# A two-layer decoder trunk on one core: in the second attention, exponentials issued ahead of copies and maxima in a row, with the groups placed anew

## The chip, the core and the metric

The kernel runs on one core of one Trainium2 chip. A core has a tensor engine (PE, with its weight loads PEld beside it), a vector engine (DVE), a scalar engine (ACT), GpSimd (POOL) and a queue engine (SP) that here issues most of the DMAs. The metric is the device time of one execution in microseconds (us). Three runs of the kernel before took 973.27, 973.38 and 973.73 us; their median, 973.38 us, is the time before.

## What is computed

The program takes 256 tokens of width 1024 through two layers. Each layer has a half-step SwiGLU feed-forward block, a token mixer, and a second half-step block; a vector `c` gives every sub-layer a shift, a scale and a gate. The mixer of layer 0 is a differential attention of 8 heads, that of layer 1 a forgetting attention of 16 heads over keys and values that were computed once before it:

```python
def block(args):                       # layer 0: two score maps per head
    logits = einsum('bqhmd,bkhmd->bhmqk', qb, k) * scale + bias
    p = softmax(where(rel >= 0, logits, -inf))
    w = p[:, :, 0] - lam * p[:, :, 1]
    return einsum('bhqk,bkhe->bqhe', w, v)
...
def block(args):                       # layer 1: one score map per head, and a decay
    logits = einsum('bqhd,bkhd->bhqk', qb, k) * scale + (F_q - F_k)
    p = softmax(where(causal, logits, -inf))
    return einsum('bhqk,bkhd->bqhd', p, v)
...
x = x + 0.5 * g1 * swiglu(h, w_in0, w_out0)
x = x + g2 * mix(h)
x = x + 0.5 * g3 * swiglu(h, w_in1, w_out1)
```

## The kernel before

**Products in three parts.** The stream `x`, the hidden rows and the weights are each kept as a rounded high part and a low part that holds the rest. A product is three matmuls into one bank (`mm3`): high by high, low weight by high, high weight by low. So each 128x1024 piece of weights (`raw`, 512 KB, loaded by SP) passes twice through the vector engines: ACT casts it (`wh<-raw`), and DVE subtracts the high part (`wl<-raw,wh`). There are 360 such pieces. `raw` has 6 buffers, `wh` 6, `wl` 5; a load into a `raw` buffer waits until both have read it, and a new `wh` or `wl` waits until PE has used the piece 6 or 5 places earlier. A second stream, `ada`, gives the shifts, scales and gates: one DVE pass over 128x1024 each.

**What sets the order.** The class `InOrder` (line 54) records what is called on PE, ACT, DVE and SP and keeps each engine's instructions in that order on the chip. It also keeps a rough clock for each engine. When an ACT or DVE call would wait by that clock, it calls a filler first: `fill_act` puts casts there, `fill_dve` subtractions or `ada` blocks. `plainly` (line 69) runs a function with the filler off. `bg`, called after matmuls by `work`, adds casts and subtractions too.

**First attention** (`attention_a`, line 975). Heads go through `group(t)` (line 1086): scores of head t, transposes of the weights of head t-1, values of t-2, and transposes of the output of t-3 on PE, then on ACT and DVE the copies, `exps` (four row maxima on DVE, each with its exponential on ACT), `squares` and `out_split`. `combine(t)` scales and subtracts the two maps (`nl`) before `group(t+1)` transposes them. Between the groups PE gets steps of projections: of the queries and keys, and, for the last three groups, of the output (`OutProj.steps`, three matmuls a step, banks `pw`). `OutProj.finish` (line 828) then does the last two heads and updates `x`.

**Second attention** (`attention_b`, line 1222). Two heads make a pair c; eight pairs go through `group(t)` (line 1320), t from 0 to 9:

- PE: `scores(t)` into two banks `sb`, `values(t-2)` into the second half of `wb`, then `weights_t(t-1)`, six transposes into `wa` and `wb`.
- ACT before the change: the high part of the output of pair t-2 (`obh<-wb`), then the four exponentials of pair t (`d<-d,nmb`), then the copy `wta<-wa` of pair t-1.
- DVE: the four maxima of pair t (`d<-sb,d` with `nmb`), the copy `wtb<-wb`, the low part `obl` of the output.
- `scale(t)` (a reciprocal `rsb` and four multiplications of `d`) is called before the last two steps ahead of `group(t+1)`.

The tiles `d` start as decays: POOL loads each of the 16 from DRAM (`d<-fdram`, line 1240) and adds a causal mask by a second DMA (`d<-tri`, line 1248), which waits for the first. Decays and masks of pairs 0 to 4 are issued ahead, those of pairs 5, 6 and 7 in groups 1, 2 and 3, one behind the other on POOL's queue.

Between the groups PE takes steps from `fills()` (line 1343): first the projections of the last two query tiles (`lq`, banks of the pool `mm`; six matmuls for every two steps, 32 steps), then six rounds of `OutProj.steps` (`pw`, three matmuls a step, 48 steps). `pw` has four banks in the same pool of four: the first two were those of the second-last projection, `pw2` and `pw3` are those of the last one, and so wait until `late_out` has drained it (ACT `lcol<-lq`, DVE `lt<-lq`, ACT `q<-lt`). The tuple of line 1353 says how many steps stand ahead of each group; four more follow the last, and eight are left to `finish`.

Of the kernel before, what the change touches and what calls it, by code (L numbers as in the profile page):

```python
# [10 lines left out]
F32 = mybir.dt.float32  # L11
# [3 lines left out]
ALU = mybir.AluOpType  # L15
# [7 lines left out]
AH = 8  # L23
# [80 lines left out]
def trunk(ctx, tc, a, out):  # L104
# [3 lines left out]
    act = InOrder(tc, nc.scalar, 0.13, 1 / 1200)  # L108
    dve = InOrder(tc, nc.vector, 0.08, 1 / 960)
# [19 lines left out]

    mm = pe.matmul  # L130


    crow = ap_.tile([P, 2, D], F32, tag="ada", name="crow").rearrange("p a b -> p (a b)")
    act.dma_start(crow[:1, :D], a["c"])
# [840 lines left out]
    def attention_a():  # L975
# [21 lines left out]
        op = OutProj(o)  # L997
# [11 lines left out]
        def exps(hd, sb):  # L1009
            g = gs[hd]  # L1010
            nl = []
            nm = kp.tile([P, 4], F32, tag="nm", name=f"nm{hd}")
            sm = kp.tile([P, 4], F32, tag="sm", name=f"sm{hd}")
            for m in range(2):
                s = sb[m]
                n_ = cp_.tile([P, 384], F32, tag=f"hidh{4 + 2 * (hd % 2) + m}", name=f"nl{hd}_{m}")
                nl.append(n_)
                for qt, (c0, w) in enumerate(QT):
                    cc = 2 * m + qt
                    dve.tensor_tensor_reduce(  # L1020
                        n_[:, c0:c0 + w], s[:, c0:c0 + w], g[:, S - w:], -0.125, BIG,
                        ALU.add, ALU.min, accum_out=nm[:, cc:cc + 1])
                    act.activation(n_[:, c0:c0 + w], n_[:, c0:c0 + w], AF.Exp,
                                   bias=nm[:, cc:cc + 1], scale=-1.0,
                                   accum_out=sm[:, cc:cc + 1])
            st[hd], sms[hd] = nl, sm
# [54 lines left out]
        def out_split(hd, pz):  # L1081
            oh, ol = o[hd]
            act.activation(oh, pz, AF.Identity, scale=subg)
            dve.scalar_tensor_tensor(ol, pz, subg, oh.bitcast(F32), op0=ALU.mult, op1=ALU.subtract)

        def group(t):

            hs, hw, hv, ho = (h if 0 <= h < AH else None for h in (t, t - 1, t - 2, t - 3))
            bank = bbank(f"po{t}") if hv is not None or ho is not None else None
            sb = scores(hs) if hs is not None else None  # L1090
            pw = weights_t(hw) if hw is not None else None
            if hv is not None:
                values(hv, bank[:, :256])
            if ho is not None:
                out_t(ho, bank[:, 256:])
            if hw is not None:
                wt = cp_.tile([P, 384], F32, tag=f"hidh{8 + hw % 2}", name=f"wt{hw}")
                act.copy(wt, pw[:, :384])
                st[hw] = wt
            if hs is not None:  # L1100
                exps(hs, sb)
            if hv is not None:
                squares(hv, bank[:, :256])
                inv_rms(hv)
            if ho is not None:
                out_split(ho, bank[:, 256:])

        def after(t):
            if t < AH:
                combine(t)  # L1110
            if 0 <= t - 2 < AH:
                scale_o(t - 2)

# [36 lines left out]
    op, rest = attention_a()  # L1150
# [71 lines left out]
    def attention_b():  # L1222
# [27 lines left out]
        r = late_pairs("wq", q[:2], None, AF.Exp)  # L1250
# [5 lines left out]
        op = OutProj(o)  # L1256
# [56 lines left out]
        def out_split(c, po):  # L1313
            if c % 2 == 0:
                o_tiles(c // 2)
            oh, ol = o[c]
            act.copy(oh, po)
            return lambda: dve.tensor_tensor(ol, po, oh.bitcast(F32), op=ALU.subtract)

        def group(t):  # L1320

            cs, cw, cv = (c if 0 <= c < NP else None for c in (t, t - 1, t - 2))
            sb = [sbank(f"sb{t}_{m}") for m in range(2)] if cs is not None else None
            ta = abank(f"wa{t}") if cw is not None else None
            tb = bbank(f"wb{t}") if cw is not None or cv is not None else None
            if cs is not None:
                scores(cs, sb)
            if cv is not None:
                values(cv, tb[:, 256:])
            if cw is not None:  # L1330
                weights_t(cw, ta, tb)
            low = out_split(cv, tb[:, 256:]) if cv is not None else None
            if cs is not None:
                exps(cs, sb)
            if cw is not None:
                weights_out(cw, ta, tb)
            if low:
                low()
            if cw is not None and t + 4 < NP:
                decay(t + 4)  # L1340
                masked(t + 4)
# [8 lines left out]
                    yield  # L1350

        fill = fills()
        for t, n in enumerate((3, 9, 8, 8, 8, 8, 7, 7, 6, 4)):
            for i in range(n):
                if 1 <= t <= NP and i == n - 2:
                    scale(t - 1)
                next(fill)
            group(t)
# [5 lines left out]
    op, rest = attention_b()  # L1364
# [132 lines left out]
```

## Time and profile before

| what | value |
|---|---|
| time, median of 3 runs | 973.38 us (973.27 to 973.73) |
| the profiled execution's own time | 973.79 us |
| its span, first to last instruction | 972.0 us |
| instructions | 20418 |
| granted PE clock | 0.997 of full speed |
| read from HBM | 264.75 MB |
| first attention's last groups and steps | about 280 to 300 us |
| second attention's groups | about 730 to 775 us |

The span lies within the profiled execution's time; 1.8 us of that time are outside it, and that execution was 0.4 us longer than the median run. A row of the timeline gives the start, the duration, the engine, the line (99 for all that `InOrder` records), the operation, the tiles out<-in, the shape, how many, and in brackets the idle time just before it with what ended it. Matmuls overlap, so the distance of two starts says more than a duration. SP, ACT or POOL followed by q is an engine's queue.

### The profile page before, as it was taken

The page shows a single profiled execution, that of the slowest core. Times are in us where ns is not written, and L with a number is a line of the kernel's source. Part 1 is how long each engine was busy: PE and PEld are TensorE (multiplying, and loading weights), DVE is VectorE, ACT ScalarE, POOL GpSimd, SP SyncE. Part 2 cuts the span into 40 slices and gives each one's busy share as a digit, 9 for nine tenths or more (in the row PEclk, how much of TensorE's full clock was granted, in tenths as well). Part 3 has the DMA queues.
Part 4 walks back from the last instruction along what each step waited for, and adds up shares of the span by engine and source line. Part 5 has one row for each costly group of instructions (what it writes and reads, how often), then busy time and mean ns, then how long its engine had stood idle before and what let it go on. Part 6 is the DMA issues. An engine that isn't in the chain of part 4 may idle for free.

```text
span 972.0 us, 20418 instructions
## 1 busy us (share of the span) xinstructions
PE 959.7 (99%) x8076; PEld 933.5 (96%) x8076; DVE 819.8 (84%) x1372; ACT 551.8 (57%) x894; POOL 74.6 (8%) x110
## 2 busy tenths in 40 slices
PE   8999999999999999999999999999999999999997
PEld 7999999998999999999998999999998899999997
DVE  6989979889999999888889988988977799555575
ACT  4466635566777654545576545445567776455432
POOL 0000200000112000000000000000044214300000
PEclk9999999999999999999999999999999999999999
DMA  9998899967866699888959799988899537977651
GB/s 360 415 356 267 326 369 344 344 228 265 314 226 229 204 376 381 306 271 311 326 197 370 289 340 338 361 295 317 315 301 224 146 111 233 262 157 267 187 153 44
DMA packets 73825, 270.32 MB, mean 278 GB/s; under 512 B 9673, under 2 KB 14577, under 8 KB 63618
## 3 DMA queue, kind: packets, MB, share of 16 engines
q1 hardware_dynamic: 66016, 259.69, 76.0%
q0 software_dynamic: 7424, 9.02, 4.3%
q8 instruction: 63, 1.03, 0.4%
q10 hardware_dynamic: 290, 0.32, 0.1%
q14 instruction: 32, 0.26, 0.1%
HBM read 264.75 MB, written 2.66 MB: 275 GB/s over the span
## 4 chain that ended last, share of the span: by engine, by line
PE 94%; DVE 3%; issue 1%; ACT 1%; POOL 0%; ACTq 0%; DVEq 0%; POOLq 0%
PE po L99 25%; PE pg L99 21%; PE pu L99 21%; PE pf L99 5%; PE pv L99 5%; PE lp L99 4%; PE pqk L99 3%; PE pw L99 3%; PE pk L99 1%; PE lq L99 1%; DVE wl L99 1%; PE wb L99 1%; DVE HL L99 1%; PE s L99 1%; PE sb L99 1%
## 5 line engine op out<-in xcount | busy, mean ns | idle before, releaser
L99 ACT CAST wh<-raw 128x1024 fp32r<-128x1024 f32 (+1 forms) x360 | 347.5, 975 | 208.4 <-PE pu L99 83.6
L99 DVE TENSOR_TENSOR wl<-raw,wh 128x1024 fp32r<-128x1024 f32 (+1 forms) x360 | 398.7, 1126 | 70.7 <-ACT sg L99 19.2
L99 DVE CUSTOM_DVE_ANT_0 ada<-ada,cact,vecs 128x1024 f32<-128x1024 f32 x160 | 203.6, 1279 | 0.4 <-DMA ada<-in_ada 0.4
L99 PE MATMUL pg<-HH,wl 128*128 128x256 f32 x608 | 168.0, 276 | 0.2 <-DVE wl L99 0.2
L99 PE MATMUL pg<-HH,wh 128*128 128x256 f32 x608 | 168.0, 276 | 0.0
L99 PE MATMUL pu<-HH,wh 128*128 128x256 f32 x608 | 167.9, 276 | 0.0
L99 PE MATMUL pg<-HL,wh 128*128 128x256 f32 x608 | 167.9, 276 | 0.0
L99 PE MATMUL pu<-HL,wh 128*128 128x256 f32 x608 | 167.9, 276 | 0.0
L99 PE MATMUL pu<-HH,wl 128*128 128x256 f32 x608 | 167.9, 276 | 0.0
L99 PE MATMUL po<-hidh,wh 128*128 128x256 f32 x528 | 145.7, 276 | 0.0
L99 PE MATMUL po<-hidh,wl 128*128 128x256 f32 x528 | 145.7, 276 | 0.0
L99 PE MATMUL po<-hidl,wh 128*128 128x256 f32 x528 | 145.7, 276 | 0.0
L99 PEld LDWEIGHTS pg<-HH,wh 128*128 128x128 f32 x608 | 114.1, 188 | 0.7 <-issue 0.6
L99 PEld LDWEIGHTS pg<-HH,wl 128*128 128x128 f32 x608 | 114.1, 188 | 0.5 <-DVE wl L99 0.4
L99 PEld LDWEIGHTS pu<-HH,wl 128*128 128x128 f32 x608 | 114.1, 188 | 0.0
L99 PEld LDWEIGHTS pu<-HL,wh 128*128 128x128 f32 x608 | 114.1, 188 | 0.0
L99 PEld LDWEIGHTS pu<-HH,wh 128*128 128x128 f32 x608 | 114.1, 188 | 0.0
L99 PEld LDWEIGHTS pg<-HL,wh 128*128 128x128 f32 x608 | 114.1, 188 | 0.0
L99 PEld LDWEIGHTS po<-hidh,wh 128*128 128x128 f32 x528 | 99.1, 188 | 0.0
L99 PEld LDWEIGHTS po<-hidh,wl 128*128 128x128 f32 x528 | 99.1, 188 | 0.0
L99 PEld LDWEIGHTS po<-hidl,wh 128*128 128x128 f32 x528 | 99.1, 188 | 0.0
L99 ACT CAST hidh<-hf 128x512 fp32r<-128x512 f32 x44 | 27.3, 621 | 41.8 <-DVE hf L99 41.6
(224 smaller groups left out, 1866.2 us busy)
## 6 DMA issues: line engine op xcount, KB each, us to landing
raw<-in_win SPq DMA_DIRECT2D x176, 512.0 KB, 6.6
ada<-in_ada SPq DMA_DIRECT2D x79, 1024.0 KB, 7.1
raw<-in_wout SPq DMA_DIRECT2D x48, 384.0 KB, 5.4
raw<-in_wout SPq DMA_DIRECT2D x48, 320.0 KB, 5.6
raw<-in_wqk SPq DMA_DIRECT2D x16, 512.0 KB, 5.5
raw<-in_wo SPq DMA_DIRECT2D x16, 512.0 KB, 6.0
raw<-in_wlast SPq DMA_DIRECT2D x16, 512.0 KB, 4.3
raw<-in_wv SPq DMA_DIRECT2D x8, 512.0 KB, 6.9
```

Source lines behind the costliest of these rows:

```text
L99: return self.tc.keep_in_program_order(f(*args, **kw))
```

## The change

Three things change, all in what is called when; no operation is added or taken away.

- **Second attention, order within a group.** The exponentials and maxima of pair t are called first and with both fillers off, then the copies `wta` and `wtb`, then the output's high and low part. So ACT has the exponentials ahead of `wta` and `obh`, and no subtraction stands between the four maxima.
- **Second attention, places.** The steps ahead of groups 0 to 9 go from (3, 9, 8, 8, 8, 8, 7, 7, 6, 4) to (3, 9, 7, 7, 8, 8, 7, 7, 7, 5). Both make 68.
- **First attention, last head.** `exps`, `combine` and `out_split` of head 7 are called with the fillers off.

```diff
+    def plain(f, *args):
+
+        r = []
+        act.plainly(lambda: dve.plainly(lambda: r.append(f(*args))))
+        return r[0]
...
             if hs is not None:
-                exps(hs, sb)
+                plain(exps, hs, sb) if hs == AH - 1 else exps(hs, sb)
...
             if ho is not None:
-                out_split(ho, bank[:, 256:])
+                plain(out_split, ho, bank[:, 256:]) if ho == AH - 1 else out_split(ho, bank[:, 256:])
 
         def after(t):
             if t < AH:
-                combine(t)
+                plain(combine, t) if t == AH - 1 else combine(t)
...
             oh, ol = o[c]
             act.copy(oh, po)
-            return lambda: dve.tensor_tensor(ol, po, oh.bitcast(F32), op=ALU.subtract)
+            dve.tensor_tensor(ol, po, oh.bitcast(F32), op=ALU.subtract)
...
-            low = out_split(cv, tb[:, 256:]) if cv is not None else None
             if cs is not None:
-                exps(cs, sb)
+                plain(exps, cs, sb)
             if cw is not None:
                 weights_out(cw, ta, tb)
-            if low:
-                low()
+            if cv is not None:
+                out_split(cv, tb[:, 256:])
...
-        for t, n in enumerate((3, 9, 8, 8, 8, 8, 7, 7, 6, 4)):
+        for t, n in enumerate((3, 9, 7, 7, 8, 8, 7, 7, 7, 5)):
```

Three places show what this does to the instructions.

**Around group 4 of the second attention, PE.** `pw0` to `pw2` are banks of the output projection, `sb4` the scores of pair 4, `wb4` and `wa4` its group's other banks. Before:

```order
L99 MATMUL pw1_9706<-obl0_9579,wh_9347 128x256
L99 MATMUL pw2_9707<-obh0_9578,wh_9347 128x256
L99 MATMUL pw2_9707<-obh0_9578,wl_9418 128x256
L99 MATMUL pw2_9707<-obl0_9579,wh_9347 128x256
L99 MATMUL pw0_9705<-obh0_9578,wh_9347 128x256
L99 MATMUL pw0_9705<-obh0_9578,wl_9418 128x256
L99 MATMUL pw0_9705<-obl0_9579,wh_9347 128x256
L99 MATMUL sb4_0_9733<-kT_6358,q2_9230 128x128
L99 MATMUL sb4_1_9734<-kT_6358,q2_9230 128x128
```

And PE there in the changed kernel:

```order
L99 MATMUL pw1_9712<-obl0_9593,wh_9347 128x256
L99 MATMUL sb4_0_9721<-kT_6358,q2_9230 128x128
L99 MATMUL sb4_1_9722<-kT_6358,q2_9230 128x128
L99 MATMUL sb4_0_9721<-kT_6358,q2_9230 128x256
L99 MATMUL sb4_1_9722<-kT_6358,q2_9230 128x256
L99 MATMUL wb4_9724<-wta2_9662,vb_6359 64x256
L99 MATMUL wb4_9724<-wtb2_9663,vb_6359 64x256
L99 MATMUL wb4_9724<-wta2_9662,vb_6359 64x128 x2
L99 MATMUL wa4_9723<-tri_1167,d6_9399 128x128 x3
L99 MATMUL wa4_9723<-tri_1167,d7_9401 128x128
L99 MATMUL wb4_9724<-tri_1167,d7_9401 128x128 x2
L99 MATMUL pw2_9713<-obh0_9592,wh_9347 128x256
```

The whole of group 4 now stands ahead of the first use of `pw2`. Group 3 moved too: six matmuls of the last `lq` projection that stood ahead of it follow it now.

**Pair 7 of the second attention, DVE.** `d14` and `d15` are the two heads' tiles, `nmb7` their maxima (a read of the accumulator follows each), `rsb7` the reciprocal that opens `scale(7)`. Before, from the first maximum on:

```order
L99 ISA d_9678,nmb_9956<-sb_0_9935,d_9678 128x128
L99 ISA nmb_9956 128x1
L99 TENSOR_TENSOR wl<-raw,wh 128x1024
L99 ISA d_9678,nmb_9956<-sb_0_9935,d_9678 128x256
L99 ISA nmb_9956 128x1
L99 ISA d_9680,nmb_9956<-sb_1_9936,d_9680 128x128
L99 ISA nmb_9956 128x1
L99 ISA d_9680,nmb_9956<-sb_1_9936,d_9680 128x256
L99 ISA nmb_9956 128x1
L99 COPY wtb_9971<-wb_9938 128x256
L99 TENSOR_TENSOR obl_9891<-wb_9938,obh_9890 128x256
L99 RECIPROCAL rsb_9987<-smb_9957 128x4
```

DVE of the changed kernel, from the second maximum on:

```order
L99 ISA d_9672,nmb_9947<-sb_0_9929,d_9672 128x256
L99 ISA nmb_9947 128x1
L99 ISA d_9674,nmb_9947<-sb_1_9930,d_9674 128x128
L99 ISA nmb_9947 128x1
L99 ISA d_9674,nmb_9947<-sb_1_9930,d_9674 128x256
L99 ISA nmb_9947 128x1
L99 COPY wtb_9958<-wb_9932 128x256
L99 TENSOR_TENSOR obl_9899<-wb_9932,obh_9898 128x256
L99 TENSOR_TENSOR wl<-raw,wh 128x1024
L99 RECIPROCAL rsb_9984<-smb_9948 128x4
```

The subtraction that stood between the maxima stands between `obl` and the reciprocal. (In pairs 5 and 6 it stands behind the maxima and ahead of `wtb`, in pairs 2 to 4 between `wtb` and `obl`.)

**Head 7 of the first attention, DVE.** `nl_0` and `nl_1` are the two maps, `nm` their maxima, `ss` the sums of squares of an earlier head. Before:

```order
L99 ISA nl_0_3649,nm_3647<-s_0_3630,g_3477 128x128
L99 ISA nm_3647 128x1
L99 TENSOR_TENSOR wl<-raw,wh 128x1024
L99 ISA nl_0_3649,nm_3647<-s_0_3630,g_3477 128x256
L99 ISA nm_3647 128x1
L99 ISA nl_1_3658,nm_3647<-s_1_3631,g_3477 128x128
L99 ISA nm_3647 128x1
L99 ISA nl_1_3658,nm_3647<-s_1_3631,g_3477 128x256
L99 ISA nm_3647 128x1
L99 ISA ada,modall<-ada,cact,vecs 128x1024
L99 ISA modall 128x1
L99 TENSOR_SCALAR ss_3664<-ss_3664 128x2
```

And in the changed kernel:

```order
L99 ISA nl_0_3649,nm_3647<-s_0_3630,g_3477 128x256
L99 ISA nm_3647 128x1
L99 ISA nl_1_3654,nm_3647<-s_1_3631,g_3477 128x128
L99 ISA nm_3647 128x1
L99 ISA nl_1_3654,nm_3647<-s_1_3631,g_3477 128x256
L99 ISA nm_3647 128x1
L99 TENSOR_TENSOR wl<-raw,wh 128x1024
L99 TENSOR_SCALAR ss_3660<-ss_3660 128x2
L99 SCALAR_TENSOR_TENSOR ol_2565<-po_3629,small,oh_2561 128x256
L99 RECIPROCAL rs_3689<-sm_3648 128x4
```

The four maxima are together, the subtraction follows them, and the `ada` block is gone from here: it now stands some 15 us later, behind the last low part `ol` and ahead of the first update of `x`; the subtraction that was ahead of that update follows it.

## The prediction

> **What bounds the kernel now.** I read the busy times first, then PE's list of waits.
>
> ```profile
> PE 959.7 (99%) x8076; PEld 933.5 (96%) x8076; DVE 819.8 (84%) x1372; ACT 551.8 (57%) x894; POOL 74.6 (8%) x110
> ```
>
> PE is busy for 959.7 of the 972.0 us and loses no matmul by the change. Only time in which PE stands can be won, and the change reaches three of the waits in PE's list (us, times, longest):
>
> ```profile
> PE pw L99 <- DVE lt L99: 1.1, 1, 1.1
> PE pw L99 <- DVE nl L99: 0.8, 2, 0.4
> PE wb L99 <- ACT wta L99: 0.6, 1, 0.6
> ```
>
> Together that is 2.5 us, 0.26% of the time. So the question is whether each goes, and what is late next. For scale: about 0.2% (1.95 us) is what a measurement of this kernel can tell from no change.
>
> **Second attention, the wait for `lt`.** PE's timeline, then ACT's and DVE's, around group 3:
>
> ```profile
> 747.44 0.28 PE L99 MATMUL lq<-HL,wh 128*128 128x258 f32 x1
> 748.14 0.28 PE L99 MATMUL pw<-obl,wh 128*128 128x256 f32 x1
> 749.48 0.38 PE L99 MATMUL pw<-obh,wh 128*128 128x256 f32 x1 [1.06 <-DVE lt L99]
> 749.70 0.28 PE L99 MATMUL pw<-obh,wl 128*128 128x256 f32 x1
> ...
> 746.31 0.37 ACT L99 CAST obh<-wb 128x256 fp32r<-128x256 f32 x1 [1.81 <-PE wb L99]
> 746.58 0.41 ACT L99 ACTIVATE d<-d,nmb 128x128 f32<-128x128 f32 x1
> 748.35 0.56 ACT L99 COPY wta<-wa 128x512 f32<-128x512 f32 x1
> 748.81 0.22 ACT L99 COPY lcol<-lq 128x1 f32<-128x1 f32 x2
> ...
> 749.00 0.76 DVE L99 TENSOR_TENSOR lt<-lq,r 128x256 f32<-128x256 f32 x2 [1.30 <-ACT lcol L99]
> 751.01 1.01 DVE L99 TENSOR_SCALAR d<-d,rsb 128x128 f32<-128x128 f32 x4
> ```
>
> The last `lq` matmul ends at 747.72, but ACT reaches `lcol` only at 748.81: `obh` had waited 1.81 us for PE's values, with the exponentials and `wta` queued behind it. `lt` follows, then `pw2`. PE's starts are 1.34 us apart where two of a run are 0.12 apart, and the next distance is 0.22: the wait costs 1.22 + 0.10 = 1.3 us.
>
> Two things remove it. The exponentials no longer queue behind `obh`, and group 3 comes six matmuls (0.7 us) earlier against the same end of `lq`. Its scores start at 743.0, the first exponential runs at 744.3, `wta` 1.77 later (748.35 - 746.58) at 746.1 and `obh` at 746.6. So ACT is idle when `lq` ends; `lcol` runs at about 747.8, `lt` at 748.0. And PE has group 4 to do ahead of `pw2`, over 2 us. Late instead could be the transposes of pair 3 in group 4: their scaling is queued on DVE behind the two `lt`, starts at about 748.8 and ends 1.01 later, at 749.85; PE comes to the second head's transposes at about 750.4. So 0.5 us is spare. Bounds 0 and -1.3; I take **-1.3**.
>
> At nothing I cost the casts. Behind `obh` of groups 2 and 4 two now stand in a row, two times 0.95 us from about 742.2 and 752.6, done 0.2 to 0.4 us ahead of the next exponentials. If that cover goes, the idle second of ACT ahead of `lcol` takes up the first pair, and 1 us of spare in the scaling of pair 5 the other.
>
> **Second attention, the wait for `wta`.** PE stood ahead of group 8:
>
> ```profile
> 762.71 0.37 PE L99 MATMUL pw<-obh,wh 128*128 128x256 f32 x1
> 765.28 0.93 PE L99 MATMUL sb<-kT,q 64*128 64x128 f32 x8
> 766.14 0.43 PE L99 MATMUL wb<-wta,vb 128*64 128x256 f32 x1
> 766.94 0.66 PE L99 MATMUL wa<-tri,d 128*128 128x128 f32 x4
> 767.57 0.37 PE L99 MATMUL pw<-obh,wh 128*128 128x256 f32 x1
> 769.60 0.28 PE L99 MATMUL pw<-obl,wh 128*128 128x256 f32 x1
> 770.51 0.43 PE L99 MATMUL wb<-wta,vb 128*64 128x256 f32 x1 [0.64 <-ACT wta L99]
> ```
>
> The distance 769.60 to 770.51 is 0.91, where a change of kind takes about 0.2: 0.7 us lost. Let T be the start of pair 7's scores. The group takes 767.57 - 765.28 = 2.29, and the seven steps that now follow it 765.28 - 762.71 = 2.57. So group 8 begins at T + 4.86 and its transposes, behind the values (766.94 - 766.14 = 0.80), at T + 5.66. `wta` is ready by T + 3.6, so this wait goes. But DVE is late now:
>
> ```profile
> 759.11 0.41 DVE L99 TENSOR_TENSOR obl<-wb,obh 128x256 fp32r<-128x256 f32 x1
> 759.44 1.21 DVE L99 TENSOR_TENSOR wl<-raw,wh 128x1024 fp32r<-128x1024 f32 x1
> 760.57 0.17 DVE L99 RECIPROCAL rsb<-smb 128x4 f32<-128x4 f32 x1
> 766.29 0.29 DVE L99 CUSTOM_DVE_ANT_0 d<-sb,d 128x128 f32<-128x128 f32 x1
> ```
>
> Maxima start at T + 1.0 (766.29 against 765.28), exponentials at T + 1.35 for 1.77, then `wta` (0.46), `obh` (0.37) and `obl`, at T + 4.0. Ahead of the scaling stand `obl` (0.33 to the next start) and the moved `wl` (1.13): the reciprocal comes at T + 5.45, the scaling 0.2 later; its first head is done at T + 6.15, its second at T + 6.65. PE waits from T + 5.66 about 0.5 for the first, 0.1 for the second, and loses 0.1 on the restart. 0.7 goes and 0.7 comes: **0**, with bounds -0.7 (the wait gone) and +0.5 (half a `wl` later). In groups 2 to 6 the `wl` stands ahead of `obl`, where DVE waits for `obh` anyway, and PE comes 1 us or more after the scaling.
>
> **The masks.** Group 7 begins about 2.0 us earlier (1.3, and two steps of 0.34 less ahead of it), T = 763.3, and its first maximum wants `d14`, mask and all, at 764.3. The mask's issue on POOL and its landing (last figure, us), then the landing of pair 6's masks, and two subtractions:
>
> ```profile
> 760.32 2.47 POOL L1248 DMA_DIRECT2D d<-tri  x2 [2.97 <-DMA d<-fdram]
> d<-tri POOLq DMA_DIRECT2D x2, 128.0 KB, 5.4
> ...
> d<-tri POOLq DMA_DIRECT2D x2, 128.0 KB, 3.6
> ...
> 739.55 1.22 DVE L99 TENSOR_TENSOR wl<-raw,wh 128x1024 fp32r<-128x1024 f32 x1
> ```
>
> Before, it landed at 760.32 + 5.4 = 765.7, 0.6 ahead of its maximum. It waits only for the DMAs ahead of it on POOL's queue, so an earlier PE doesn't bring it. At 765.7 it would be 1.4 us late, and all of that late for PE in group 8. What changes is the weight loads beside these DMAs, since a load is issued when a `wl` ends. The slow mask had one issued 0.3 us behind it (the `wl` of 759.44 ends at 760.65); that `wl` now comes at about 760.5. The `wl` of 739.55 moves to 741.3, so that its load meets less of pair 5's decay, first of the chain. I expect the chain 1 to 2 us earlier and the last mask in 3.6 to 4.5 us, landed between 763 and 764.5: **0**. Bounds 0 and +1.4.
>
> The Trainium skill's page "DMA: Bandwidth & Descriptors", section "Queues, rings and completion order", says that each DMA engine takes turns between its queues a packet at a time; 5.4 against 3.6 us agrees. Its section "Anatomy of one DMA — SWDGE (gpsimd) path" gives 2.0 us and the bytes at 436 GB/s, an estimate of 2.3 us for 128 KB; by that price no mask is late and the sum is the same, but both rows are longer.
>
> **First attention, the wait for `nl`.**
>
> ```profile
> 287.64 0.28 PE L99 MATMUL pw<-ol,wh 128*128 128x256 f32 x1
> 288.33 0.30 PE L99 MATMUL pw<-tri,nl 128*128 128x128 f32 x1 [0.42 <-DVE nl L99]
> 289.02 0.44 PE L99 MATMUL pw<-tri,nl 128*128 128x128 f32 x2 [0.39 <-DVE nl L99]
> ```
>
> Two distances of 0.69, less 0.2 and 0.12 for a change and a run, with a restart inside: 0.95 us lost by the starts, 0.81 by the idle times; I take the starts, on which PE's pace rests. The `wl` between the maxima held ACT's second exponential by its 1.13 us; without it `nl` is 1.1 earlier and both waits go: -0.95. But the `ada` block comes back ahead of the updates of `x`, and their sums run one behind the other on POOL:
>
> ```profile
> 301.18 0.87 DVE L99 SCALAR_TENSOR_TENSOR x<-pw,modall,x 128x256 f32<-128x256 f32 x2
> 302.50 0.49 ACT L99 ACTIVATE HH<-x,modall 128x256 fp32r<-128x256 f32 x1
> 304.72 4.42 POOL L443 TENSOR_TENSOR acc<-acc,sq 128x256 f32<-128x256 f32 x5 [0.53 <-ACT sq L99]
> ...
> 323.26 1.22 DVE L99 TENSOR_TENSOR wl<-raw,wh 128x1024 fp32r<-128x1024 f32 x1
> 325.18 0.28 PE L99 MATMUL pg<-HH,wl 128*128 128x256 f32 x1
> ```
>
> DVE has no gap from the last `ol` to the second update, now with about 1.2 us more in it: that update starts at 301.8 (0.2 later), and ACT's `HH` from it at 302.3 instead of 302.50. The sums, then three `wl`, the rescaling and the rows of `h` follow from there, so this chain gains 0.2 where PE gains 0.95. The `wl` of 323.26 ended at 324.48, 0.7 ahead of its first use; now 324.3 against 324.2. PE waits 0.1 and restarts for 0.1: **-0.75**, with bounds -0.95 and -0.5 (the chain no earlier at all).
>
> **The sum.** -1.3 + 0 + 0 - 0.75 = -2.05. The profiled execution took 973.79 (span 972.0, 1.8 around it) and would take 971.74; it was 0.41 above the median run, so the median goes from 973.38 to **971.3**. Behind both places PE, DVE and ACT have their old order, and buffers that PE frees set their pace, so the gain lasts to the end.
>
> **The rivals.**
>
> - *The mask is late.* The chain of decays and masks keeps its old times, and 1.4 of the gain becomes a wait of DVE's maxima, then of PE's transposes in group 8: 972.7, or between 971.6 and 972.7 in part. For it: a chain on one queue that no engine feeds. Against it: the loads that move. Chance 0.27.
> - *The first attention gives back more*, or group 4 waits for its scaling: half a us to one, 971.9 to 972.3 (I take 971.9, the nearer end). Margins of 0.1 and 0.5 us speak for it. Chance 0.1.
> - *Better:* the group 8 wait goes too, as DVE finds time for the `wl` early; 971.3 - 0.7 = 970.6. Against it: the new order puts it behind `obl`. Chance 0.1.
> - *Slower:* moved weight loads meet two more transfers of the chain, each 1.8 us longer (5.4 - 3.6): landing at 765.7 + 3.6 = 769.3, 5.0 late, 976.3. It decides from a landing of 766.35 on, where the gain of 2.05 is used up, and shows as slower from 768.3. Against it: as many loads as before. Chance 0.04.
> - That the change doesn't do what it says is excluded by the order of the rows.
>
> **How the numbers follow.** The forecast has 0.49, with 0.4 us to either side. Some six in ten of it lie below 971.43, with all of the better case: faster 0.4, slower 0.04, same 0.56. The range goes from the better case to a mask a little later than before: 970.4 to 973.2.
>
> **What would show it.** PE's list without `lt` and `nl`, and `wa` waiting for DVE's `d` instead of `wb` for `wta`, 0.5 to 0.7 us: right. A wait of DVE's `d` for a DMA at group 7, with a mask that lands after 764.5: the first rival. A wait of `pg` for `wl` near 324 above 0.3 us: the second. Wrong in any case: PE still waiting near 748, or new idle time of PE in the last feed-forward.

## The result, and the profile after

| | median | lowest to highest | runs |
|---|---|---|---|
| before, beside the change | 973.82 us | 973.04 to 977.45, and one run of 1369 | 22 |
| changed kernel | 978.87 us | 972.11 to 989.17 | 22 |

The ratio is 1.005 [1.0031, 1.0068]: the change makes the kernel 0.5% slower, where 0.2% faster was forecast, and the time lies outside the range. The runs of 1369 and 989.17 us count as slow and are left out of the ratio. The wide spread of the others belongs to the result: four of them lie below 975.3, 972.11 the lowest, and seven between 981.5 and 985. The profiled execution took 978.58 us, 4.8 more than that of before.

PE's list of waits in the changed kernel (us, times, longest), the lines that the rest goes by:

```profile
PE wb L99 <- DVE obl L99: 2.9, 1, 2.9
...
PE pg L99 <- DVE wl L99: 0.6, 2, 0.4
PE wb L99 <- DVE rsb L99: 0.6, 1, 0.6
PE wa L99 <- DVE d L99: 0.4, 1, 0.4
```

The three waits that the change was to remove are gone. In their place stands one of 2.9 us at group 8 of the second attention and some small ones. The place is best seen as a table by stage, around groups 7 to 9. The columns are the stretch, its length, the busy time of PE, PEld, DVE, ACT and POOL, the granted clock, the DMA share and GB/s. First before, then after:

```profile
764.00:769.00 5.00, 5.00 (x46) 4.23 (x46) 3.96 (x17) 3.69 (x13) 0.00 (x0) 1.00 0.47 71
769.00:772.00 3.00, 2.36 (x23) 1.85 (x21) 1.48 (x6) 1.45 (x7) 0.00 (x0) 1.00 0.48 164
772.00:778.00 6.00, 6.00 (x54) 5.55 (x53) 4.02 (x7) 5.08 (x9) 0.00 (x0) 1.00 0.27 87
```

```profile
764.00:769.00 5.00, 4.38 (x39) 3.72 (x35) 1.99 (x9) 0.51 (x2) 1.11 (x1) 1.00 0.81 161
769.00:772.00 3.00, 0.12 (x2) 0.00 (x0) 1.66 (x9) 3.00 (x11) 0.00 (x0) 0.89 0.01 3
772.00:778.00 6.00, 5.94 (x29) 5.11 (x29) 4.12 (x9) 2.31 (x4) 0.00 (x0) 0.50 0.27 87
778.00:785.00 7.00, 7.00 (x62) 6.48 (x62) 4.23 (x8) 5.02 (x10) 0.73 (x1) 0.99 0.45 144
```

PE stands almost the whole of 769 to 772. Then, although it is busy for 5.94 of 6.00 us, it does 29 matmuls where it did 54: the granted clock is 0.50. What it had stood for is told by DVE's timeline (first a maximum of pair 6, then the first one of pair 7) and by POOL's:

```profile
761.85 0.29 DVE L99 CUSTOM_DVE_ANT_0 d<-sb,d 128x128 f32<-128x128 f32 x1 [1.68 <-DMA d<-tri]
...
768.52 0.29 DVE L99 CUSTOM_DVE_ANT_0 d<-sb,d 128x128 f32<-128x128 f32 x1 [2.57 <-DMA d<-tri]
771.49 0.42 DVE L99 TENSOR_TENSOR obl<-wb,obh 128x256 fp32r<-128x256 f32 x1 [1.33 <-ACT obh L99]
```

```profile
756.43 2.15 POOL L1245 DMA_DIRECT2D d<-fdram  x2
762.64 2.47 POOL L1253 DMA_DIRECT2D d<-tri  x2 [4.05 <-DMA d<-fdram]
```

The first maximum of pair 7 is computed when its mask has landed; behind it come the other maxima, ACT's exponentials, `wta` and `obh`, and the `obl` for which PE waits. The mask was issued at 762.64, when the decays of 756.43 had landed, and needed 5.7 us (the list of transfers gives it as the last figure):

```profile
d<-tri POOLq DMA_DIRECT2D x2, 128.0 KB, 5.7
```

It landed at 768.36. Pair 7's scores began at 763.42, so by PE the maximum was ready to run at 764.42: 3.9 us late. (DVE itself, which pair 6's late mask had held up, was free from 765.95 on.)

To see where the time went I set the start of each matmul of the changed kernel against the matmul of the same number before:

```
at      after - before   what lies between
 277 us   -0.99          start-up, code that the change leaves alone
 290      -2.06          the two waits for nl gone: -1.07
 308      -1.58          PE held up by x at 305:    about +0.5
 326      -0.75          a new wait for wl at 324:  about +0.8
 734      -0.75
 749.5    -1.19          a wait in group 1 (+0.8), the wait for lt gone (-1.27)
 765      -0.52          pair 6's mask late at group 7: 0.6
 772      +2.69          pair 7's mask late at group 8: +3.2
 778      +4.60          clock 0.50: +1.9
 end      +4.69
```

In this execution all of the loss, and more, is the late mask and the clock behind it. The queue was late from its first masks on: the third one issued landed at 732.05 (729.35 before), 0.1 ahead of the maximum of pair 0's second head on DVE, which had stood 1.36 us, and that is the wait in group 1. But no part of this table reaches the runs at 981.5 to 985 us, so I looked for a second cause too.

### The profile page after: what moved, and what is told of

Read it like the earlier page. It is cut to its first block, busy times and chain, and to the rows that moved or that the text cites. A ratio compares the mean times of both kernels' runs of the same rounds, so it can differ in the third digit from the quotient of the medians.

```text
span 976.7 us, 20425 instructions
## 1 busy us (share of the span) xinstructions
PE 962.2 (99%) x8076; PEld 934.5 (96%) x8076; DVE 819.8 (84%) x1372; ACT 552.5 (57%) x894; POOL 74.4 (8%) x110
## 4 chain that ended last, share of the span: by engine, by line
PE 92%; DVE 4%; issue 2%; DMA 1%; ACT 1%; POOL 0%; SPq 0%; DVEq 0%; ACTq 0%; POOLq 0%
PE po L99 25%; PE pg L99 21%; PE pu L99 21%; PE pf L99 5%; PE pv L99 5%; PE lp L99 4%; PE pqk L99 3%; PE pw L99 3%; PE pk L99 1%; PE lq L99 1%; DVE wl L99 1%; DVE HL L99 1%; DVE ada L99 1%; DMA ada<-in_ada 1%; PE s L99 1%
## 5 line engine op out<-in xcount | busy, mean ns | idle before, releaser
L99 ACT CAST hidh<-hf 128x512 fp32r<-128x512 f32 x44 | 27.3, 621 | 41.4 <-DVE hf L99 41.2
```

Source lines behind the costliest of these rows:

```text
L99: return self.tc.keep_in_program_order(f(*args, **kw))
```

## The experiments

Two theories were set against each other from the start, and both proved to be needed. **Masks:** the chain of decays and masks on POOL's queue doesn't follow PE; the last mask comes late, PE stands, and the clock drops. **Pace:** a new short wait of PE ahead of a feed-forward lets all the matmuls behind it run a little further apart. Where the expectations use letters, M is the theory of the masks, and the others are forms of the second. A third possibility, that some moved work costs something in itself, was tried along by doing the two parts of the change apart. Each ratio is to the runs of the kernel before that stood beside it on the same chip.

**1. The late masks left out.** In the changed kernel pairs 5 to 7 get no mask.

```diff
                 decay(t + 4)
-                masked(t + 4)
```

> The changed kernel without the six mask transfers of pairs 5 to 7 (their decays stay), so that these pairs are not masked. Theory M (the late masks alone cost what the change loses, by DVE's maxima, PE standing ahead of group 8 and the low clock behind it): PE stands nowhere ahead of groups 7 and 8 for more than 0.8 us, no low clock at 770 to 778, 971.5 to 973 us, ratio 0.9975 to 0.999, and all runs within 1.5 us. Theory O (the new order and places cost the time whatever the masks do): 977 to 979 us with PE still standing about 3 us ahead of group 8.

Measured: 982.69 us (976.61 to 985.84, 12 runs), 1.0062 [1.0041, 1.0082]. PE doesn't stand at groups 7 and 8, and yet the kernel is no faster. The theory of the masks alone falls. The profile shows the second cause in its barest form. Stages of nothing but matmuls of 256 columns, in the two feed-forwards, first before and then this kernel:

```profile
330.00:400.00 70.00, 70.00 (x620) 70.00 (x620) 66.45 (x87) 37.05 (x43) 0.00 (x0) 1.00 0.95 353
820.00:890.00 70.00, 70.00 (x620) 70.00 (x619) 41.29 (x43) 34.82 (x39) 11.91 (x21) 1.00 0.88 238
```

```profile
330.00:400.00 70.00, 70.00 (x596) 70.00 (x596) 65.17 (x85) 35.45 (x42) 0.00 (x0) 1.00 0.95 345
820.00:890.00 70.00, 70.00 (x597) 70.00 (x596) 41.70 (x43) 33.68 (x38) 16.01 (x28) 1.00 0.89 229
```

PE is busy without a gap and the granted clock is 1.00 in all four rows, but it does 620 matmuls in one kernel and 596 in the other. Their starts are 113.3 ns apart in the one and 117.8 in the other (a row's count holds a few that reach into its stretch from outside). In all 20 profiles these stages show one of the two values, and the pace, once taken, holds from matmul to matmul over the stage. Behind the first attention that is some 1440 matmuls, so 1440 x 4.45 ns = 6.4 us; in the last feed-forward about 980, so 4.4 us. I call the two the close and the wide pace.

**2. The late masks added by POOL itself.** Its add needs no DMA queue, and POOL is idle otherwise.

```diff
-                nc.gpsimd.dma_start(diag, m2, accum_op=ALU.add)
+                if c < 5:
+                    nc.gpsimd.dma_start(diag, m2, accum_op=ALU.add)
+                else:
+                    nc.gpsimd.tensor_tensor(diag, diag, m2, op=ALU.add)
```

> The changed kernel with the masks of pairs 5 to 7 added by POOL itself (six additions of 128x256) in place of six transfers; the result is the same. Theory M: an addition takes about 0.9 us as POOL's sums of squares do, so the chain of three pairs gets 6 to 9 us shorter and pair 7's mask is there 4 us or more ahead of its maximum; 971.5 to 973.5 us, ratio 0.998 to 0.9995. If decays alone are late (rival D: it is the transfers of the decays, not those of the masks, that the loads delay): d14 still lands after 764, 975 to 978 us. Theory O: 977 to 979 us.

Measured: 972.49 us (971.81 to 981.26), 0.9993 [0.9972, 1.0013]. Eight of the 12 runs lie at 971.8 to 972.7, three at 976.1 to 976.9, one at 981.26. The long wait is gone from PE's list, and at group 8 this is left:

```profile
PE wa L99 <- issue: 0.4, 1, 0.4
```

So with the masks in time the change can come out below the kernel before, in two runs of three: 972.4 at the median of the eight, against 973.2 for the lower group of before beside them. That is 0.8 us, not the 2.05 of the forecast. The three runs some 4 us higher are of the size that the last feed-forward makes at the wide pace.

**3. All masks added by POOL.** As in 2, without the condition.

> The changed kernel with all 16 masks added by POOL. Theory M: as the run with pairs 5 to 7, and the wait of 0.4 us for pair 0's scaling at 734.4, which a late mask of the second head makes, goes too: 971 to 973 us, 0.3 to 0.6 us below that run. Against it: DVE and POOL might hinder each other from 717 to 735, where the additions would stand beside DVE's subtractions; then DVE's mean for a subtraction rises above 1.13 us and the gain goes.

Measured: 976.44 us (972.78 to 978.65), 1.0009 [0.9989, 1.0028], above the 971 to 973 expected, though no mask is late. The profiled execution has the last feed-forward at the wide pace, so the median tells mostly which pace most runs took. But the hindrance is there too. One subtraction that ran beside five of POOL's adds took 4.43 us, where its neighbours take 1.22:

```profile
724.92 3.49 POOL L1253 TENSOR_TENSOR d<-d,tri 128x256 f32<-128x256 f32 x5
725.08 4.43 DVE L99 TENSOR_TENSOR wl<-raw,wh 128x1024 fp32r<-128x1024 f32 x1 [0.61 <-PE lp L99]
```

From 717 to 742 us PE loses 0.25 in this profile, so this isn't what made the time.

**4. The first attention's part alone**, put into the kernel before (`plain` and its three calls).

```diff
-                exps(hs, sb)
+                plain(exps, hs, sb) if hs == AH - 1 else exps(hs, sb)
...
-                out_split(ho, bank[:, 256:])
+                plain(out_split, ho, bank[:, 256:]) if ho == AH - 1 else out_split(ho, bank[:, 256:])
...
-                combine(t)
+                plain(combine, t) if t == AH - 1 else combine(t)
```

> The kernel before with the change's first-attention part alone. By the prediction: 0.75 us less, 973.0 against 973.8, ratio 0.9992. By the trace of the changed kernel (theory F: PE gains 1.07 us at head 7's transposes and gives all of it back by 326, since the ada block that now stands ahead of the updates of x holds the sums of squares and the weights behind them): between 0 and 0.3 us more, ratio 1.0000 to 1.0003, with PE waiting for wl at 324 to 326.

Measured: 979.18 us (973.81 to 984.57), 1.0034 [1.0009, 1.0059]. The smallest part of the change, which I had put down as -0.75, is alone enough to make the kernel slower, and by more than the 0.3 us of theory F. Its runs come in groups at about 974, 978, 980.5 and 984, which 4.4 and 6.4 us, apart and together, would make. Its profile shows the wide pace begin in the last feed-forward, at a wait that the kernel before has too:

```profile
800.85 0.28 PE L99 MATMUL pg<-HH,wh 128*128 128x256 f32 x1
801.35 0.39 PE L99 MATMUL pg<-HH,wl 128*128 128x256 f32 x1 [0.22 <-DVE wl L99]
801.58 0.28 PE L99 MATMUL pg<-HL,wh 128*128 128x256 f32 x1
...
802.16 0.28 PE L99 MATMUL pu<-HH,wl 128*128 128x256 f32 x1
802.28 0.28 PE L99 MATMUL pu<-HL,wh 128*128 128x256 f32 x1
802.40 0.28 PE L99 MATMUL pu<-HH,wh 128*128 128x256 f32 x1
```

Ahead of the wait the distances are 0.113, behind it 0.118; and so they stay up to about 910.

**5. The second attention's part alone**: the changed kernel with the three calls of the first attention as they were.

> The change without its first-attention part. Theory R (a matmul of 256 columns follows the last one after 113 ns or after 118 ns; a stretch keeps its pace, and each wait of PE for a weight piece inside a stretch decides it anew; the first-attention part adds such a wait at 324, ahead of some 1450 like matmuls, so up to 6.4 us): no wait of PE near 324, 113 ns from 326 to 487 in the trace, no run in the band 6 us above the fastest; times in two groups, 972 and 976 to 977, by the last feed-forward as before, and 1 to 5 us more where a mask is late; median 972 to 976, ratio 0.998 to 1.002. If the late masks alone make the loss: 978 to 979, as the whole change.

Measured: 977.09 us (971.79 to 980.87), 1.0014 [0.9989, 1.0038]. So this part alone isn't faster either. The median is above the 972 to 976 of theory R, and six runs lie 6 us or more above the fastest, where it expected none; experiment 14 shows what late masks alone add. The profiled execution is one of the quick ones, with the mask in time. The rows that correspond to those of the changed kernel above:

```profile
759.17 2.47 POOL L1253 DMA_DIRECT2D d<-tri  x2 [3.44 <-DMA d<-fdram]
```

```profile
d<-tri POOLq DMA_DIRECT2D x2, 128.0 KB, 3.3
```

Issued 3.5 us earlier and, by the list, 2.4 us faster, it landed at 762.24, 2.0 us ahead of its maximum. The chain from the first decay of pair 5 to this landing is the same code in every kernel that keeps the transfers, and yet takes anything from 21.8 to 27.3 us: 21.8 here, 25.4 before, and 26.2, 26.8 and 22.5 in three profiles of the changed kernel.

**6. The wait at 802 removed.** In both feed-forwards behind an attention, one piece of weights is cast and subtracted ahead of the last step of the hidden rows instead of behind it. In the kernel before only the last feed-forward had a wait there.

```diff
                         mh.go(2 if k < 6 else 1)
+            cp_part()
+            sub_part()
             mh.go(2)
```

> The kernel before, with one weight piece in each of the two feed-forwards behind an attention cast and subtracted two rows of h earlier (about 1.5 us), so that PE need not wait for it near 802. Theory R: no wait there, 113 ns through the last feed-forward in every run, so the group of runs near 977 goes, all runs within about 1 us, 972.6 to 973.2, ratio 0.996 to 0.9995 against runs of before with both groups. If the pace has nothing to do with that wait: 0.4 us less (the wait itself) and about a third of the runs near 977 as before.

Measured: 973.41 us (972.77 to 976.05), 0.9988 [0.9973, 1.0003]. Eleven of the 12 runs are below 974.1, and one is at 976.05. Of the 35 runs of the kernel before beside experiments 5 to 8, 12 were above 976. The wait is gone from the profile, and with it the upper group but for that one run. The interval reaches 1, so it is the counts that speak for the theory of the pace, and those of experiment 13 join them.

**7. The changed kernel with the early piece.** The edit of 6.

> The whole change with the same two pieces earlier, so that PE waits neither at 324 (0.4 to 0.6 us in the changed kernel) nor at 806. Theory R: 113 ns in both feed-forwards in every run; what is left above 971.5 us is the late mask of pair 7 (5.4 us in the profiled execution of the change: 3.2 of standing, 2.1 of low clock): times from 971 to 977, median 972 to 976, ratio 0.997 to 1.002. If the masks alone make the loss: unchanged, 978 to 979.

Measured: 979.65 us (972.58 to 983.88), 1.0048 [1.0024, 1.0072]. That is above theory R's range, and eight of the 12 runs are above its 977: the waits for weight pieces are taken out, and the loss stays. In the profile the mask is late:

```profile
PE wb L99 <- DVE obl L99: 3.8, 1, 3.8
```

**8, 9 and 11. The changed kernel with the early piece and POOL's adds for pairs 5 to 7**, the edits of 2 and 6: once timed, then two more profiles.

> The same with the masks of pairs 5 to 7 added by POOL. Theory R with the masks out of the way: no long wait of PE anywhere, all runs within 1.5 us, 970.5 to 972 us, ratio 0.995 to 0.998: below both kernels. If a group 4 or 6 us higher remains, the pace is set by something else than waits for weight pieces.

> A second look at the change with the early pieces and POOL's masks, whose runs fell in two groups, 971.0 to 971.5 and 977.3 to 978.0 us, for where the 6.2 us of the upper group lie. Theory R1 (the first feed-forward behind an attention, 1440 matmuls by 4.35 ns = 6.3 us, still falls into the pace of 118 ns without a wait for a weight piece): 118 ns from 319 or 324 to 487. Theory R2 (another stretch, the feed-forward from 537 to 715, 1560 matmuls, 6.8 us): 118 ns there. In a run of the lower group: 113 ns in all three.

> A third look at the change with early pieces and POOL's masks, for the same question: in the upper group 118 ns from 319 or 324 to 487 (R1) or from 537 to 715 (R2), in the lower group neither.

Measured: 977.49 us, four runs at 971.0 to 971.5, seven at 977.3 to 978.0, one at 980.4; 1.0013 [0.9991, 1.0035]. The profiles took 971.0, 978.72 and 971.77. Neither a late mask nor the wait at 802 is left, and two groups remain, 6.3 us apart, where one was expected. The slow one of the three profiles runs at the wide pace from 318 to 493:

```profile
330.00:400.00 70.00, 70.00 (x597) 70.00 (x596) 65.17 (x86) 36.01 (x42) 0.00 (x0) 1.00 0.94 342
```

So a third place sets a pace, behind the first attention. In this profile PE has no wait for `wl` near 324, where the changed kernel's has; its only one of that stage is at 305, for DVE's update of `x`.

**10 and 12. The changed kernel, two more profiles.**

> A second look at the changed kernel. Theory R and M together: a wait of PE for wl of 0.3 to 0.7 us near 324 in every execution; behind it 113 or 118 ns to 487, as it falls (0 or 6.3 us); a late mask of pair 7 with 2 to 4 us of standing at 769 and the low clock behind it; 113 or 118 ns behind a wait near 802 (0 or 4.3 us). The time is 971.5 plus what of these the trace shows, within 1 us.

> A third look at the changed kernel, as the second: 971.5 us plus 6.3 if 118 ns holds from 324 to 487, plus 4.3 if it holds through the last feed-forward, plus what a late mask costs at 769 to 778, within 1 us.

Measured: 979.08 and 981.07 us. The two are slow for different reasons. In the first the mask is late:

```profile
PE wb L99 <- DVE obl L99: 3.6, 1, 3.6
```

In the second it is in time, and the pace is wide from a wait at 327 on (6.3 us):

```profile
330.00:400.00 70.00, 70.00 (x597) 70.00 (x596) 65.64 (x87) 35.99 (x41) 0.00 (x0) 1.00 0.94 345
```

Both also lost 1.7 us between 59 and 109 us, in the first feed-forward, which ran at the wide pace there; the change leaves that code alone. With the start-up, which differs by 1.3 us between the two, this is why the expected sum misses the second by 3 us.

**13. The second attention's part alone, with the early piece and POOL's adds**: the edits of 2, 5 and 6 together.

> The second-attention part of the change alone, with the two early weight pieces and POOL's masks for pairs 5 to 7. Theory F (the first-attention part sets the pace of 118 ns, by a wait of PE at 305 for x or at 324 for a piece): nothing of that here, all runs in one group within 1.5 us, 971.0 to 972.0 us (the kernel before with early pieces, 973.4, less 1.3 for lt and less 0.7 for wta), ratio 0.996 to 0.998. Theory S (the pace comes from the second attention or from chance in every kernel): a group 6 us higher stays, 977 to 978.

Measured: 972.29 us (971.50 to 973.68), 0.9975 [0.9965, 0.9986]. All 12 runs lie in one group, 2.2 us wide. It is faster than the kernel before, by a quarter of a per cent. How much of that is the order and the places, and how much the early piece (0.9988 in experiment 6) or POOL's adds, isn't shown: the kernel before with those two alone was not run. Of the three causes none is left, and PE's list, apart from the start-up, holds the old wait for `nl`, and 0.6 us at group 8:

```profile
PE pw L99 <- DVE nl L99: 0.8, 2, 0.4
PE wa L99 <- issue: 0.6, 1, 0.6
```

**14. The same with the masks by DMA**: the edits of 5 and 6.

> The same with the masks by transfers, as in the change. Theory F with M: 971 us where the mask is in time, up to 977 where it is 3 to 4 us late (its standing and 2 us of low clock); no run above 978; median 973 to 977. If masks cost nothing by themselves: as the run with POOL's masks.

Measured: 975.84 us (971.32 to 980.07, 11 runs, one of 1605 left out), 1.0005 [0.9983, 1.0027]. Against 13 only the masks differ, so at the median they cost 975.84 - 972.29 = 3.6 us. (Two runs lie above the expected 978.) Its list of waits, and the two stretches around the wait:

```profile
PE wb L99 <- DVE obl L99: 3.9, 1, 3.9
```

```profile
766.00:771.00 5.00, 1.10 (x12) 0.93 (x10) 2.14 (x11) 3.22 (x11) 0.00 (x0) 0.99 0.04 5
771.00:778.00 7.00, 7.00 (x48) 5.68 (x49) 4.54 (x11) 3.45 (x7) 0.00 (x0) 0.77 0.27 85
```

PE does 12 matmuls in the first five us, and the clock granted in the next seven is 0.77 on average.

**15. The new order with the old places of the groups**: 14 with the old tuple.

```diff
-        for t, n in enumerate((3, 9, 7, 7, 8, 8, 7, 7, 7, 5)):
+        for t, n in enumerate((3, 9, 8, 8, 8, 8, 7, 7, 6, 4)):
```

> The same with the old places of the groups (3, 9, 8, 8, 8, 8, 7, 7, 6, 4): the order of the second attention alone, and early pieces. Group 7 then begins 0.7 us later, and PE reaches pw2 at 748 with two steps less of cover. If the places bring the lateness of the masks: fewer late runs than with the new places, median 972 to 974. If the order does: as with the new places, 973 to 977.

Measured: 974.2 us (eight of 11 runs up to 974.45, the others 976 to 980), 0.9999 [0.9982, 1.0016]. The wait for `lt` is back:

```profile
PE pw L99 <- DVE lt L99: 0.9, 1, 0.9
```

So the order within a group doesn't remove it: the places are needed. Whether they would do it alone was not run. The groups that come later also seem to meet their masks in time more often: eight of 11 runs are below 974.5 here, four of 11 in 14, which so few runs don't prove. In the profile the mask landed at 761.65, 4.8 us ahead of its maximum.

**16, 17 and 18. The first attention's part alone with the early piece**, the edits of 4 and 6: once timed, then two more profiles.

> The first-attention part of the change alone, with the two early pieces: PE waits at neither 324 nor 802. Theory F: the wait at 305 for x is still there in some executions, times in two groups, 972 to 973 and 978 to 979, median in either, ratio 0.999 to 1.005. If the wait for the piece at 324 alone set the pace: one group, 972.4 to 973.2, ratio 0.996 to 0.999.

> A second look at the first-attention part with early pieces (times in two groups, 972 to 974 and 978.5 to 981). Theory F: a trace of the upper group shows 118 ns a matmul from about 319 to 490 and a wait of PE for x near 305; a trace of the lower group shows 113 ns there, with the wait or without it. If the wait at 305 has nothing to do with it: an upper trace without that wait.

> A third look at the same kernel, with the same expectations: 118 ns from 319 to 490 and a wait for x near 305 in the upper group, 113 ns in the lower one.

Measured: 974.03 us, seven runs at 972.1 to 974.1 and five at 978.5 to 980.9; 1.0011 [0.999, 1.0032]. The profiled execution of 16 took 973.62 us, the other two 979.14 and 979.01. Their stage behind the first attention, 16 first, then 18:

```profile
330.00:400.00 70.00, 70.00 (x620) 70.00 (x619) 67.59 (x91) 37.36 (x44) 0.00 (x0) 1.00 0.96 356
```

```profile
330.00:400.00 70.00, 70.00 (x596) 70.00 (x596) 65.15 (x86) 35.65 (x42) 0.00 (x0) 1.00 0.93 342
```

The 5.4 us between them are mostly that stage: 620 matmuls against 596 in the same 70 us. Against 6 only the first attention's part differs. PE's timeline of 18 has the wait at 305, 0.45 from start to start; before's has 0.13 at the same two matmuls:

```profile
305.45 0.28 PE L99 MATMUL lg<-HL,wh 128*128 128x258 f32 x1
305.90 0.39 PE L99 MATMUL lg<-HH,wh 128*128 128x258 f32 x1 [0.16 <-DVE x L99]
```

```profile
307.70 0.29 PE L99 MATMUL lg<-HL,wh 128*128 128x258 f32 x1
307.83 0.28 PE L99 MATMUL lg<-HH,wh 128*128 128x258 f32 x1
```

Where PE comes there at the wide pace, as in the changed kernel, the same `x` holds it up by 0.18 only.

Taken together, the runs with neither a late mask nor the wait at 802 divide by the first attention's part: without it (6 and 13) none of 24 is above 976.1, with it (8 and 16) 13 of 24 are above 977.3.

## Why the prediction was wrong

**What was right.** The wait for `lt` was to give 1.3; the starts of PE give 1.27, though of the two things named the order alone leaves 0.9 of the wait (experiment 15). Group 8 was to come out at 0, with the transposes waiting for the scaling: they wait 0.36 us in experiment 2 and 0.63 in 13. The two waits for `nl` were to give 0.95; they give 1.07, and the sum that gave 0.95 (two distances of 0.69 less 0.2 and 0.12) comes to 1.06. The second attention as a whole is a draw even with its last mask in time: from 717 to 790 us it comes out 0.9 to 1.1 us shorter than before's in experiments 5, 2 and 12, but 0.2 and 0.5 us longer in 9 and 13.

**The step on the masks failed:** "I expect the chain 1 to 2 us earlier and the last mask in 3.6 to 4.5 us, landed between 763 and 764.5". It landed at 768.36, in 5.7. I had read one execution's chain as its length and drawn a gain from where two weight loads move; the profiles show that the length varies by 5.5 us, by 4.3 in three of the changed kernel itself. I had also left out what stands ahead of the chain on its queue: of the 2.7 us by which the mask lands later than before, 1.9 had been lost on the masks and decays of pairs 0 to 4 (the first decay of pair 5 is issued at 742.13 against 740.26). The first rival, the late mask with chance 0.27, has the mechanism. The landing is nearly that of the slower case, 769.3, to which I gave 0.04; but that moved weight loads delayed it, as I had it there, no run shows, and what sets a transfer's time stays open. Experiment 14 beside 13 shows that the lateness isn't a rarity: 3.6 us at the median.

**A term was missing behind it, the clock.** A mask 3.9 late makes PE stand 3.2, and then 1.9 more go at half clock, up to 778. Before, PE's longest wait here was 1.1, so no row showed it. The same in experiments 7 and 14: standing 4.0 and 4.2 from start to start and a mean clock of 0.54 and 0.77 in the seven us from 771. The granted clock is 0.50 from 771.3 to 778.2 in the changed kernel, from 770.9 to 774.3 in 14, and in 10 from 774.7 to 778.1, though PE had begun again at 773.0 there. The Trainium skill, page "TensorE: Matmul & The Clock Gate", section "Part 1: The HAM clock gate (the "warmup" mystery)", says that the clock halves after an idle window of about 3.4 us and that this window runs freely. The traces agree that it halves and that its times aren't tied to the wait's; on the length they differ, since here 2.9 us without a matmul were enough.

**The first attention's term failed at "this chain gains 0.2 where PE gains 0.95".** The code ahead of both places ran 0.99 earlier in the changed kernel's profile. Against that, ACT's second `HH` comes 0.95 later than before (302.46 against 302.50), not 0.2 earlier, and the `wl` of 323 comes 0.77 later (323.04 against 323.26). I had followed DVE alone. The moved `ada` block completes `modall`, and ACT waits for it; behind that wait stand a table load and a cast, and only then the first `HH` of `x`. ACT in the changed kernel, then the first of these rows before:

```profile
299.26 0.21 ACT L99 CAST HH<-modall 128x16 fp32r<-128x16 f32 x1 [1.89 <-DVE modall L99]
299.49 1.28 ACT L99 ACT_TABLE_LOAD   x1
300.78 1.05 ACT L99 CAST wh<-raw 128x1024 fp32r<-128x1024 f32 x1
301.74 0.51 ACT L99 ACTIVATE HH<-x,modall 128x256 fp32r<-128x256 f32 x1
```

```profile
299.32 0.20 ACT L99 CAST HH<-modall 128x16 fp32r<-128x16 f32 x1
```

All 14 profiles with the first attention's part have this wait of ACT, 1.88 or 1.89 us, and none of the six without it. What it does to PE, 20 us later:

```profile
323.04 1.22 DVE L99 TENSOR_TENSOR wl<-raw,wh 128x1024 fp32r<-128x1024 f32 x1
```

```profile
323.60 0.28 PE L99 MATMUL pg<-HH,wh 128*128 128x256 f32 x1
324.31 0.39 PE L99 MATMUL pg<-HH,wl 128*128 128x256 f32 x1 [0.43 <-DVE wl L99]
```

PE, 2.06 earlier than before at the end of the groups, loses 0.5 up to 308, at the first update of `x`, which I hadn't seen at all, and 0.8 at 324, where I had 0.2. From -0.99 to -0.75, the part comes out at +0.24 instead of -0.75, and at 0.19 to 0.25 in all seven profiles that have it without the early piece. The size is the lesser error. The greater is that I priced a wait by its length alone. Each of these two stands ahead of some 1440 like matmuls that can run 113 or 118 ns apart: 0 or 6.4 us.

**The forecast took one profile for the kernel.** Both feed-forwards of before's profile were at the close pace, and its mask came 0.6 ahead of its need. The time before has two groups of its own, at 973 and at 976 to 978, which three runs don't reveal. Any step that stood 0.6 us from a wait, or put a wait ahead of a long stage, was a draw and not a sum.

**What stays open** is how a wait sets the pace. All 14 profiles with the first attention's part have the wait at 305, and none of the six without it; five of the 14 end up at the wide pace in the feed-forward behind the first attention, none of the six. Of the nine profiles with the wait near 802 three have the last one at the wide pace, of the 11 without it none. But the first feed-forward took the wide pace in 10 and 12, where the change does nothing. The distances of the matmuls near 310 repeat to a ns or two from profile to profile and go with the pace as the stage begins. Some of them (ns, from behind the two matmuls of the sums on; experiments by number):

```
                              distances                   pace on entry
before                        307 128 117 120 122          113
changed kernel, 9, 17, 18     308-309 120 120 121          118
1, 4                          305 125 120                  113
11, 12                        306 125 119                  113
10                            306 129 116                  113
```

The set of the second row is followed by the wide pace in all four of its profiles, every other set, in 16, by the close one; a second wait, for `wl` near 324, can turn either into the other (118 to 113 in the changed kernel's profile, 113 to 118 in 1 and 12). What the pace is, no run here shows, and which of a wait's properties chooses isn't known. How often each pace comes is known only as counts.

## What to carry to other kernels

- Price a wait of a saturated engine by what stands behind it as well as by its length: ahead of a long run of like matmuls, half a us went with losses of 4 to 6. Work that is moved off such an engine's path comes back at the next place that needs it, so follow it there, on every engine that waits for its result.
- A chain of transfers that no engine feeds doesn't come earlier when the engines do, and one profile doesn't tell its length. Where it is a few small tiles, an idle engine can do the work (POOL's add of 128x256 took 0.7 to 1.8 us), at a place where no subtraction of DVE is held up by it.
- Look at how the runs are spread before reading a sum from one profile: groups some us apart mean that a place decides which way it goes, and removing that place (experiments 6 and 13) can be worth as much as the waits in the list.

## What the hardware showed unexpectedly

- Matmuls of 256 columns follow each other at one of two distances, 113.3 or 117.8 ns, at a granted clock of 1.00 and with no gap, for up to 170 us. The same page of the Trainium skill, section "Wait — 56ns, not 53.3ns?", gives one distance for warm matmuls in a row, N / 2.4 GHz and 2.5 ns, an estimate of 109 ns here; both measured ones are longer.
- The same accumulating DMA of a 128 KB mask, the one for pair 7's first head, took from 3.1 us (experiment 5) to 7.3 (experiment 6).
- After a standstill of PE the granted clock was 0.50 for 3.4 us (experiments 10 and 14) or 6.8 us (the changed kernel and experiment 7), not for a time that grows with the standstill: 3.9 and 4.2 us of it in the first two, 3.2 and 4.0 in the others.
- A subtraction of DVE that ran beside five adds of POOL lasted 4.43 us instead of 1.22 (experiment 3), and two beside one add 1.54 and 1.61 (2 and 9).
